# Five more chunks of the gate blocks by seven products

## The chip, the cores and the metric

The kernel runs on one core of a Trainium2 chip. The metric is the device time of one execution in microseconds (us). Before the change it is 2385.62 us, the median of three runs (2385.2 to 2386.27).

TensorE (PE) multiplies matrices into PSUM, VectorE (DVE) and ScalarE (ACT) work element by element, GpSimd (POOL) issues some of the transfers, and SyncE (SP) issues the loads of weights. All engines run beside each other and wait for one another by semaphores.

## The reference

One decoder layer on 256 tokens of width 2048: a half-step SwiGLU FFN, then a mixer with two branches (sparse attention with an indexer, and an RG-LRU recurrence), then a second FFN, with layer norms between. What matters here is the part between the projections and the merging of the branches:

```python
q, k, v, qi, ki, wi, rx, rg, gates = split_cols(h @ w_in[l])
y_attn = dsa_attention(q, k, v, qi, ki, wi)
g_attn, g_rnn = jnp.split(jax.nn.sigmoid(gates), 2, axis=-1)
merged = g_attn * (y_attn @ w_attn_branch[l]) + g_rnn * (y_rnn @ w_rnn_branch[l])
```

The product for `gates` has K = 2048 and 4096 columns. The kernel computes it as eight blocks of 512 columns, `gate_block(0)` to `gate_block(7)`.

## The kernel before

**Products.** Activations are held with features on the partitions and serve as the stationary operand, 128x128 at a time; weights move past them. Both are float32 split into a high and a low half, and a product takes three terms (`three`, L637 to L639): high by high, high by low, low by high. `W.unit` hands out the weights in order. A weight piece (`raw`, 128x1024) is loaded by SP (L177), its high half `wh` is a copy by ACT (L228), its low half `wl` a subtraction by DVE (L229). Five pieces of `wh` and `wl` fit (`HL_BUFS`). When TensorE begins a piece, four further ones are to be split (`AHEAD`) and eight to be loaded; the raw pieces have four buffers.

**Plain and fast chunks.** K has sixteen tiles of 128, and a chunk is four of them. A plain chunk of a block of 512 columns is two pieces ("c"), and each K tile is multiplied for both halves of the tokens (t = 0, 1) with 512 columns: 4 x 2 x 3 = 24 matmuls. A fast chunk treats two token halves, two halves of the columns and pairs of K tiles as 2x2 blocks and needs seven products in place of eight, with 256 columns each: 7 x 2 x 3 = 42 matmuls. Its weights come as one load of 128x2048 (`rf`, two buffers), of which four pieces are made: "p1q3" (DVE sums 1024 columns into `ws`, L191), "p2" (a sum of 512, L195), "q5p7" (a sum of 512, L198) and "q4p6" (no sum). Three of these have 1024 columns and one has 512, and each is split by L228 and L229. The sums on the activations' side are the `forms` (tiles `sh`, `sl`), made once for chunks 2 and 3 of this stage (`FAST_A`) and used by the projection blocks before.

**PSUM.** A plain block sums into two `mm` buffers, one for each token half. A block with a fast chunk takes two more, of the four `bp` buffers, from its first fast piece until `joined` (L1135 to L1141) has added the seven products up: a copy by ACT, four sums of 256 columns and two of 512 by DVE. `joined` writes two `stg` tiles; without fast chunks ACT's tanh (L1281) reads `mm` itself.

**The order around the change.** After the FFN come nine projection blocks (`A_ORDER`; all but the first, and but the small one, with chunks 2 and 3 fast), then `gate_block(0)` to `gate_block(5)`, then four blocks of the attention branch's output (`ya`). The order on PE, SP and POOL is the order of the program; that of DVE and ACT is the scheduler's. Beside the gate blocks runs the background (`bg`): the indexer for the second token half (L1171 on PE, L1191 to L1202 on DVE) and sixteen attention heads, four at a time (`head`: scores L1215 and L1216 on PE, L1219 to L1224 on DVE, exponential L1227 on ACT, scaling L1229 and L1231 on DVE, transposes L1235 on PE, copy L1238 on ACT, value products L1241 and L1242 on PE, L1245 and L1246). Each step of these tasks is taken when TensorE begins a new piece of weights (`on_piece`), so the tasks are counted in pieces, not in time. Scores, transposes and value products of a head each take one `bp` buffer. The first four heads start in the same step; later ones one step apart. `bg.drain` after the sixth gate block would finish what is left. The gates go to memory by POOL (L1282) and are fetched for the merging after the sixth block. `left_again` (L578) prepares sums of `ya` for the next stage.

`block_plan` spreads the pieces of a block: one plain piece first, then the fast pieces with the plain ones between them. `GATE_FAST` names the fast chunks of each gate block and is read at two places, where the pieces are listed and where the block is computed.

Of the kernel before, what the change touches and what calls it, by code (L numbers as in the profile page):

```python
# [65 lines left out]
FAST_A = (2, 3)  # L66


def block_plan(chunks, fills, lead=2, n=4, late=True):

    plain = [("c", k) for q in range(n) if q not in chunks for k in (4 * q, 4 * q + 2)]
    forms = [(f, q) for q in chunks for f in FORMS]
    rest = ["o"] * fills
    plan = [(rest.pop(), 0) for _ in range(min(lead, fills))] + plain[:1]
    plain = plain[1:]
    slow = []
    while plain or rest:
        for which in (plain, rest) if late else (rest, plain):  # L80
            if which:
                p = which.pop(0)
                slow.append((p, 0) if p == "o" else p)
    if not forms:
        return plan + slow
    step = len(forms) / (len(slow) + 1)
    n = 0
    for i, f in enumerate(forms):
        plan.append(f)
        while len(slow) > n and i + 1 >= (n + 1) * step:  # L90
            plan.append(slow[n])
            n += 1
    return plan
# [14 lines left out]
FILLS = [(g, nb, 2 * p) for g, (b0, b1) in enumerate(SEGS[:-1]) for nb in range(4) for p in range(b1 - b0)]  # L108
PLANS = layer_plans()
PLAN_A = block_plan(FAST_A, 0, 0)  # L110
GATE_FAST = ((), (), (), (3,), FAST_A, FAST_A, (), ())
YA_FAST = ((), (0, 1), (0, 1), (0, 1))
YR_FAST = ((0, 1), (0, 1), (0,), (0,))
MG_FAST = ((), (0, 1), (0, 1))
# [185 lines left out]
def tile_layer(ctx, tc, x_fm, x_tm, pos, f1a, f1o, wA, wki, wB, wG, lru, wab, wrb, wo, f2a, f2o,  # L300
# [43 lines left out]
    def block_pieces(ap, plan, fills=None, fo=None):  # L344
        chunk = {}
        for f, k in plan:
            if f == "c":
                pieces.append((ap[:, k * 512:k * 512 + PIECE], None))
            elif f == "o":
                g, nb, k = next(fills)  # L350
                k += 2 * SEGS[g][0]
                pieces.append((fo[nb][:, k * 512:k * 512 + PIECE], None))
            else:
                if k not in chunk:
                    chunk[k] = ap[:, k * 2048:(k + 1) * 2048]
                pieces.append((chunk[k], f))
# [18 lines left out]
    for b in range(6):  # L375
        block_pieces(wG[b], block_plan(GATE_FAST[b], 0, 0))
    for b in range(4):
# [8 lines left out]
    for b in range(6, 8):  # L386
        block_pieces(wG[b], block_plan(GATE_FAST[b], 0, 0))
    for b in range(4):
# [882 lines left out]
    def product(x, forms, fast):  # L1271

        c, e = blockF(x, forms, block_plan(fast, 0, 0, len(x) // 4), None)
        return (joined(c, e), True) if e else (c, False)

    def gate_block(b):
        s, own = product(hs, gate_forms, GATE_FAST[b])
        dst = (ga + gr)[b]
        for t in range(2):
            u = s[t] if own else U("gt")  # L1280
            A.activation(u, s[t], AF.Tanh, scale=0.5)  # L1281
            G.dma_start(dst[t], u)  # L1282
# [220 lines left out]
```

## Time and profile before

| | us |
|---|---|
| Time, median of three runs | 2385.62 |
| Span of the profiled execution | 2383.7 |
| What lies around the span, by the median | 1.9 |
| PE busy in the span | 2367.7 |
| DVE busy in the span | 2212.6 |
| ACT busy in the span | 1504.0 |
| The six gate blocks beside the heads (906.2 to 1070.6 us) | 164.4 |
| PE busy in them | 163.84 |
| DVE busy in them | 136.01 |
| ACT busy in them | 96.42 |

The profile is of one execution, whose span runs from the first to the last instruction; its own time isn't listed beside the three runs, which lie 1.5 to 2.6 us above the span. A busy time is the time in which at least one instruction of the engine runs: matmuls overlap their successors, so the distance of two starts, not the duration of one, is what a matmul costs, and the same holds in smaller measure for DVE. The idle time of an engine is put down to what ended it. The granted clock of TensorE is 1.000 over the whole span.

### The profile page before, as it was taken

The numbers are of one execution on the slowest core, as the hardware profiler recorded it, in microseconds if no ns is written. First come the engines' busy times: TensorE is split into PE (matmuls) and PEld (weight loads), VectorE is DVE, ScalarE is ACT, GpSimd is POOL, SyncE is SP. The second block draws the span as 40 slices with busy tenths as digits, with TensorE's granted clock in tenths as the row PEclk, the third lists the DMA queues.
The fourth block names the chain that finished last, engine by engine and source line by source line (L and its number), as shares of the span: only waits on it lengthen the run. The fifth ranks groups of instructions, "written<-read, shape, count | busy, mean of one in ns | idle before, by whom it ended". The sixth has DMA issues, their size and how long they took to land.

```text
span 2383.7 us, 38855 instructions
## 1 busy us (share of the span) xinstructions
PE 2367.7 (99%) x14926; PEld 2115.5 (89%) x14926; DVE 2212.6 (93%) x3130; ACT 1504.0 (63%) x2048; POOL 124.0 (5%) x196
## 2 busy tenths in 40 slices
PE   9999999999999999999999999999999999999999
PEld 7898999989988888888999998888888899999997
DVE  8999999999999998789788888998999999999997
ACT  7666666666647554665588885555766666666663
POOL 0000000000000000001000001100000000000000
PEclk9999999999999999999999999999999999999999
DMA  8666666666666456547655568755676666676665
GB/s 302 194 226 210 219 212 227 215 213 212 201 206 221 177 186 183 185 142 264 207 184 184 190 187 295 254 191 179 213 221 216 217 211 196 230 230 207 215 214 178
DMA packets 123163, 501.26 MB, mean 210 GB/s; under 512 B 14272, under 2 KB 14528, under 8 KB 102112
## 3 DMA queue, kind: packets, MB, share of 16 engines
q1 hardware_dynamic: 104400, 454.60, 54.9%
q0 software_dynamic: 18576, 44.17, 8.0%
q8 instruction: 117, 1.92, 0.3%
q14 instruction: 70, 0.57, 0.1%
HBM read 467.26 MB, written 10.49 MB: 200 GB/s over the span
## 4 chain that ended last, share of the span: by engine, by line
PE 94%; DVE 4%; issue 1%; DMA 0%; ACT 0%; POOL 0%; POOLq 0%; SPq 0%; DVEq 0%; ACTq 0%
PE mm L637 21%; PE mm L639 21%; PE mm L638 21%; PE bp L638 6%; PE bp L637 6%; PE bp L639 6%; PE mm L1337 4%; PE mm L1335 4%; PE mm L1336 4%; DVE wl L229 2%; PE bp L1027 1%; DVE ws L191 0%; PE bp L1216 0%; PE bp L1115 0%; PE bp L1171 0%
## 5 line engine op out<-in xcount | busy, mean ns | idle before, releaser
L228 ACT ACTIVATE wh<-raw 128x1024 fp32r<-128x1024 f32 (+2 forms) x538 | 550.1, 1044 | 286.6 <-PE mm L639 162.4
L229 DVE TENSOR_TENSOR wl<-raw,wh 128x1024 fp32r<-128x1024 f32 (+2 forms) x538 | 635.0, 1197 | 95.0 <-ACT wh L228 93.1
L228 ACT ACTIVATE wh<-rf 128x1024 fp32r<-128x1024 f32 (+1 forms) x489 | 440.2, 915 | 314.4 <-PE mm L639 155.4
L229 DVE TENSOR_TENSOR wl<-rf,wh 128x1024 fp32r<-128x1024 f32 (+1 forms) x489 | 506.2, 1042 | 11.7 <-ACT wh L228 6.0
L637 PE MATMUL mm<-wh,hs 128*128 128x512 f32 (+1 forms) x884 | 317.0, 359 | 0.0
L639 PE MATMUL mm<-wh,hs 128*128 128x512 f32 (+1 forms) x884 | 311.1, 352 | 1.2 <-DVE hs L818 1.2
L638 PE MATMUL mm<-wl,hs 128*128 128x512 f32 (+1 forms) x884 | 310.8, 352 | 0.1
L639 PE MATMUL mm<-wh,g 128*128 128x512 f32 (+1 forms) x696 | 274.5, 394 | 0.0
L637 PE MATMUL mm<-wh,g 128*128 128x512 f32 (+1 forms) x696 | 274.4, 394 | 0.0
L638 PE MATMUL mm<-wl,g 128*128 128x512 f32 (+1 forms) x696 | 274.4, 394 | 0.0
L228 ACT ACTIVATE wh<-ws 128x1024 fp32r<-128x1024 f32 x163 | 173.0, 1061 | 141.1 <-PE mm L639 77.0
L637 PE MATMUL bp<-wh,sh 128*128 128x256 f32 x918 | 258.6, 282 | 0.0
L638 PE MATMUL bp<-wl,sh 128*128 128x256 f32 x918 | 256.5, 279 | 1.3 <-DVE wl L229 1.3
L639 PE MATMUL bp<-wh,sl 128*128 128x256 f32 x918 | 256.2, 279 | 0.0
L191 DVE TENSOR_TENSOR ws<-rf 128x1024 f32<-128x1024 f32 x163 | 198.6, 1218 | 7.6 <-DMA rf<-f1a 2.1
L229 DVE TENSOR_TENSOR wl<-ws,wh 128x1024 fp32r<-128x1024 f32 x163 | 198.5, 1218 | 2.8 <-ACT wh L228 2.6
L639 PEld LDWEIGHTS mm<-wh,hs 128*128 128x128 f32 x884 | 165.9, 188 | 27.5 <-DVE hs L818 2.6
L637 PEld LDWEIGHTS mm<-wh,hs 128*128 128x128 f32 x884 | 166.0, 188 | 24.3 <-issue 1.5
L638 PEld LDWEIGHTS mm<-wl,hs 128*128 128x128 f32 x884 | 166.1, 188 | 22.5 <-DVE wl L229 0.7
L1337 PE MATMUL mm<-hs,wl 128*128 128x256 f32 x640 | 179.8, 281 | 0.0
L1335 PE MATMUL mm<-hs,wh 128*128 128x256 f32 x640 | 179.8, 281 | 0.0
L1336 PE MATMUL mm<-hs,wh 128*128 128x256 f32 x640 | 179.8, 281 | 0.0
(341 smaller groups left out, 5327.0 us busy)
## 6 DMA issues: line engine op xcount, KB each, us to landing
rf<-f1a SPq DMA_DIRECT2D x64, 1024.0 KB, 5.6
rf<-f2a SPq DMA_DIRECT2D x64, 1024.0 KB, 5.8
raw<-f1o SPq DMA_DIRECT2D x88, 512.0 KB, 6.6
raw<-f2o SPq DMA_DIRECT2D x88, 512.0 KB, 6.7
raw<-wB SPq DMA_DIRECT2D x80, 512.0 KB, 4.2
raw<-wG SPq DMA_DIRECT2D x54, 512.0 KB, 4.3
raw<-f2a SPq DMA_DIRECT2D x48, 512.0 KB, 4.6
raw<-f1a SPq DMA_DIRECT2D x47, 512.0 KB, 5.4
```

The source lines that it names most:

```text
L191: v.tensor_tensor(t, b[:, 0:4:3], b[:, 1:2].to_broadcast([P, 2, 2, 256]), op=OP.add)
L228: nc.scalar.activation(hp, src, AF.Copy)
L229: self.last = nc.vector.tensor_tensor(lp, src, hp, op=OP.subtract)
L637: T.matmul(ps, xh, w[0], start=start, stop=False)
L638: T.matmul(ps, xh, w[1], start=False, stop=False)
L639: T.matmul(ps, xl, w[0], start=False, stop=stop)
L1027: T.transpose(ps[:, k * S + t * P:k * S + (t + 1) * P], z[:, t * 512 + k * P:t * 512 + (k + 1) * P], ident)
L1335: T.matmul(ps[:, :S], w[0], x[:, 0], start=first, stop=False)
L1336: T.matmul(ps[:, :S], w[0], x[:, 1], start=False, stop=False)
L1337: T.matmul(ps[:, :S], w[1], x[:, 0], start=False, stop=last)
```

## The change

One tuple changes. It says for each of the eight gate blocks which chunks of K are fast.

```diff
-GATE_FAST = ((), (), (), (3,), FAST_A, FAST_A, (), ())
+GATE_FAST = ((3,), (3,), FAST_A, FAST_A, FAST_A, FAST_A, (), ())
```

Blocks 0 and 1 take chunk 3 by seven products, block 2 chunks 2 and 3, and block 3, which had chunk 3 already, chunk 2 as well: five chunks more. In blocks 0 to 2 the `joined` path takes the place of the direct one. The pieces of a block follow from its plan: 8 without a fast chunk, 10 with one, 12 with two. The left-hand forms of chunks 2 and 3 exist already.

## The prediction

> **What bounds the kernel now.** I read the page first: the busy line of each engine, then the engines of the chain that ended last, then the two kinds of weight transfer.
>
> ```profile
> PE 2367.7 (99%) x14926; PEld 2115.5 (89%) x14926; DVE 2212.6 (93%) x3130; ACT 1504.0 (63%) x2048; POOL 124.0 (5%) x196
> PE 94%; DVE 4%; issue 1%; DMA 0%; ACT 0%; POOL 0%; POOLq 0%; SPq 0%; DVEq 0%; ACTq 0%
> rf<-f1a SPq DMA_DIRECT2D x64, 1024.0 KB, 5.6
> raw<-wG SPq DMA_DIRECT2D x54, 512.0 KB, 4.3
> ```
>
> TensorE carries 94% of the chain; VectorE, at 93% busy, is close behind. What decides is therefore the stretch that the change touches. I call the gate blocks G0 to G5 and cut the windows view where the timeline shows each block's last product. The columns are length, then busy time of PE, PEld, DVE, ACT and POOL with counts, clock, DMA share, GB/s.
>
> ```profile
> 906.20:933.50 27.30, 27.30 (x129) 20.63 (x129) 22.77 (x48) 13.51 (x18) 0.00 (x0) 1.00 0.63 196
> 933.50:959.20 25.70, 25.70 (x121) 21.06 (x120) 20.39 (x44) 13.12 (x21) 1.08 (x2) 1.00 0.62 182
> 959.20:988.30 29.10, 29.10 (x142) 24.24 (x141) 22.68 (x52) 16.80 (x41) 1.07 (x2) 1.00 0.56 182
> 988.30:1015.10 26.80, 26.44 (x154) 22.96 (x153) 22.03 (x47) 17.59 (x41) 1.08 (x2) 1.00 0.59 197
> 1015.10:1049.50 34.40, 34.21 (x213) 30.35 (x212) 29.63 (x58) 21.97 (x46) 1.07 (x2) 1.00 0.37 138
> 1049.50:1070.60 21.10, 21.10 (x135) 18.91 (x134) 18.51 (x22) 13.42 (x15) 1.07 (x2) 1.00 0.45 138
> sum 164.40, PE 163.84 PEld 138.16 DVE 136.01 ACT 96.42 POOL 5.39; mean PE 27.31 PEld 23.03 DVE 22.67 ACT 16.07 POOL 0.90
> ```
>
> PE is idle for 0.56 us of 164.40, so a product less is time gained. DVE is idle for 28.4 us: that is the cover on which the change draws. For a stretch where this cover is already used up, the same view over the fast projection blocks (745.5 to 906.2 us) ends in this sum:
>
> ```profile
> sum 160.70, PE 159.26 PEld 141.44 DVE 158.09 ACT 94.27 POOL 0.00; mean PE 22.75 PEld 20.21 DVE 22.58 ACT 13.47 POOL 0.00
> ```
>
> There DVE is 98.4% busy and PE still loses only 1.44 us of 160.70. The waits of PE from 700 to 1160 us name the three kinds of loss that follow here as well:
>
> ```profile
> PE bp L638 <- DVE wl L229: 0.7, 1, 0.7
> ...
> PE bp L1115 <- ACT rl L1182: 0.6, 1, 0.6
> PE bp L1215 <- DVE ya L1246: 0.4, 1, 0.4
> ```
>
> The first is a weight half that DVE made too late; the other two are a PSUM buffer of the `bp` kind not yet read out.
>
> **TensorE's side.** First and last of 23 consecutive 512-wide products, then of 24 consecutive 256-wide ones, from the timeline of PE:
>
> ```profile
> 914.44 0.39 PE L638 MATMUL mm<-wl,hs 128*128 128x512 f32 x1
> ...
> 919.57 0.40 PE L639 MATMUL mm<-wh,hs 128*128 128x512 f32 x1
> 903.28 0.28 PE L637 MATMUL bp<-wh,sh 128*128 128x256 f32 x1
> ...
> 905.96 0.28 PE L639 MATMUL bp<-wh,sl 128*128 128x256 f32 x1
> ```
>
> The pitch is 5.13/22 = 0.2332 us for 512 columns and 2.68/23 = 0.1165 us for 256. A plain chunk (four K tiles, two token halves, three terms) is 24 x 0.2332 = 5.60 us; a fast one (seven products, two K tiles each, three terms) is 42 x 0.1165 = 4.89. I take 0.70 saved, five times: **-3.5 us**. (A block's products then take 22.4 us plain, 21.7 with one fast chunk, 21.0 with two.) That is 0.15%. The most that the change can give is thus under 0.2%, about what a measurement of this kernel can tell from no change.
>
> **VectorE's side.** One stretch of DVE's timeline holds the kinds of instruction that a fast chunk needs, each starting as the one before it lets it (L198, the third sum, has L195's 512 columns):
>
> ```profile
> 1052.45 0.42 DVE L1138 TENSOR_TENSOR stg<-bp,stg 128x256 f32<-128x256 f32 x1
> 1052.78 0.41 DVE L1139 TENSOR_TENSOR stg<-bp,stg 128x256 f32<-128x256 f32 x1
> 1053.12 1.27 DVE L1141 TENSOR_TENSOR stg<-stg,mm 128x512 f32<-128x512 f32 x2
> 1054.31 1.22 DVE L229 TENSOR_TENSOR wl<-rf,wh 128x1024 fp32r<-128x1024 f32 x1
> 1055.44 1.22 DVE L229 TENSOR_TENSOR wl<-raw,wh 128x1024 fp32r<-128x1024 f32 x1
> 1056.58 1.22 DVE L191 TENSOR_TENSOR ws<-rf 128x1024 f32<-128x1024 f32 x1
> 1057.71 1.22 DVE L229 TENSOR_TENSOR wl<-rf,wh 128x1024 fp32r<-128x1024 f32 x1
> 1058.85 0.68 DVE L195 TENSOR_TENSOR rf<-ws,rf 128x512 f32<-128x512 f32 x1
> 1059.45 0.68 DVE L229 TENSOR_TENSOR wl<-rf,wh 128x512 fp32r<-128x512 f32 x1
> 1060.05 1.22 DVE L229 TENSOR_TENSOR wl<-raw,wh 128x1024 fp32r<-128x1024 f32 x1
> ```
>
> By the distance of the starts, 1024 columns cost 1.135 us, 512 cost 0.60, 256 cost 0.335. A plain chunk is two subtractions, 2.27. A fast one is the sums (L191 1.135, L195 0.60, L198 0.60) and three and a half subtractions (3 x 1.135 + 0.60): 6.34. Each chunk adds 4.07, five 20.3; a block's weights take 9.08 plain, 13.15 with one fast chunk, 17.2 with two. G0, G1 and G2 had no fast chunk and now need `joined` (four of 256, and L1141 twice, 1.19): 2.53 each, 7.6. Together **+27.9 us of DVE**, against 28.4 idle. ACT gets 1.5 more copies of 1024 per chunk and three small ones, some 9 us at about DVE's lengths, beside 68 idle: I cost them at nothing; were that cover gone, DVE's subtractions behind them would be late too.
>
> The sum over six blocks just fits, but it is not evenly spread. The background tasks take one step per piece of weights, and a fast chunk has four pieces where a plain one has two. G0 to G5 had 8, 8, 8, 10, 12, 12 pieces and now have 10, 10, 12, 12, 12, 12. The heads' first scores come at the 14th step and their last product at the 45th:
>
> ```profile
> 948.40 0.38 PE L1215 MATMUL bp<-hT,hT 128*128 128x128 f32 x2
> ...
> 961.29 0.55 DVE L1231 TENSOR_SCALAR s<-s,s 128x128 f32<-128x128 f32 x2
> 962.23 1.47 PE L1235 MATMUL bp<-ident,s 128*128 128x128 f32 x12
> ...
> 1043.66 0.38 PE L1242 MATMUL bp<-pT,stg 128*128 128x128 f32 x2
> ```
>
> They ended late in G4; now all of them, and the index scores before them, fall into G0 to G3. That is where DVE is short. Through G2 (32 steps) I count as follows. DVE's work other than products was 22.77 - 9.08 - 2.53 (the join of the block before) = 11.2 in G0, 20.39 - 9.08 = 11.3 in G1, 22.68 - 9.08 = 13.6 in G2, and eight of ten steps of G3, 0.8 x (22.03 - 13.15) = 7.1: 43.2. The blocks' own work is 2 x 13.15 + 17.2 and three joins, 51.1. DVE needs 94.3. PE needs 2 x 21.7 + 21.0 for products, and for the rest, its busy time less the old products, 27.3 - 22.4 = 4.9, 3.3, 6.7 and 0.8 x (26.44 - 21.7): 83.1. **DVE is short by 11.2 us at the end of G2.** What is left for G3 is 0.2 x 8.9 of its own other work and G4's 29.63 - 17.2 - 2.53 = 9.9, which with 17.2 and a join makes 31.4, against PE's 0.2 x 4.7 + (34.21 - 21.0) + 21.0 = 35.1; in G4 and G5 it is 19.7 against 21.0. So what comes later wins time back for DVE, but PE's waits are spent by then.
>
> Two things soften this. Sums for the next stage were pulled forward as filler and can go back after G3:
>
> ```profile
> L578 DVE TENSOR_TENSOR t<-ya 128x256 f32<-128x256 f32 x8 | 3.2, 415 | 0.0
> ```
>
> At 0.33 each they take 2.6. And DVE enters G0 four pieces ahead; if it lends three, at 13.15/10 to 17.2/12, about 1.4 each, that is 4.2. So 11.2 - 2.6 - 4.2 = 4.4 us in which PE waits. From below the bound is nothing (the whole lead is lent and the tasks slip past their steps unharmed, as in the projection stage); from above 11.2.
>
> **PSUM, loads, queues.** A fast block holds two of the four `bp` buffers from its second piece to its join. The first four heads go in step: their scores, transposes and value products each take all four, and now find two. On PE's hand-written order everything queues behind: the two later heads, and the block's own products. From the rows above each such wait is 0.4 to 0.6 us; three groups of two give up to 3 us, from nothing. It lies in G1 and G2, where DVE is short anyway, and a stall there lets DVE catch up, so I add only 0.1. Five transfers of 1024 KB replace ten of 512 KB on SP, the bytes are the same, and the DMA share of 0.56 to 0.63 in G0 to G3 leaves room; I cost that at nothing, hidden by the loads' eight pieces of lead. A late one would cost DVE the 1.3 us by which the larger lands later, once or twice. The output path (ACT's tanh, POOL's store) is read only after G5.
>
> **The sum**: -3.5 + 4.5 = +1.0 us. On the profiled execution this is 2383.7 to 2384.7. The median, 2385.62, is 1.92 above that span; carried over, **2386.6 us**.
>
> **A rule that speaks against.** The timeline shows 256 columns at exactly half the pitch of 512, though each product brings its own weight load:
>
> ```profile
> L639 PEld LDWEIGHTS mm<-wh,hs 128*128 128x128 f32 x884 | 165.9, 188 | 27.5 <-DVE hs L818 2.6
> ```
>
> The load, at 188 ns, is longer than the pitch of 116.5, so loads overlap. The Trainium skill, page "TensorE: Matmul & The Clock Gate", section "Back-to-back issue gap", holds that in a stream of load and product the spacing is set by both, so that short products cost more per column (81 ns for 128 columns, 131 for 512). This trace disagrees (0.1165 us against 0.2332); by the rule a fast chunk would save less than the 0.70 above, and rival 3 prices its extreme from the rows.
>
> **Rivals.**
> 1. *The cover holds.* As in the projection stage (98.4% busy, 1.44 lost), lead and filler take the whole shortage; PE waits 0 to 2.4 us. Time 2382.1 to 2384.5. For it: that stage. Against it: there the load was even, without sixteen heads.
> 2. *VectorE takes over as the bound, in G1 and G2.* The lead doesn't help, because a head's scale (961.29) is needed by PE's transposes at 962.23, hardly a microsecond later, whatever weights lie ready. Then the 11.2 are paid: -3.5 + 11.2 = +7.7, 2393.3; with the filler moved away +5.1, 2390.7. It decides, as a slowdown over 0.2%, from 8.3 us of waiting.
> 3. *The weight load sets the pace of short products.* At 188 ns a fast chunk would be 42 x 0.188 = 7.9 against 5.6, five times +2.3: 2397. The pitch above speaks against it.
> 4. *It doesn't do what it says,* because the left-hand forms for these chunks are late or the order elsewhere shifts. The projection blocks used the same forms before. Time about 2385.6, either side.
>
> **How the numbers follow.** Forecast (2384.5 to 2388.5) 0.50; rival 1 0.24; rival 2 0.22 (2388.5 to 2394); rival 3 0.01; rival 4 0.03. Faster by over 0.2% (under 2380.8) needs more than the products can give: 0.02, out of rival 4. Slower (above 2390.4): two thirds of rival 2, and rival 3: 0.16. Within 0.2%: 0.82. The range 2382.5 to 2392.0 leaves out the last of rival 1 and the upper part of rival 2.
>
> **What would show it.** Right: 15 products fewer at 0.2332 us, DVE over 95% busy from G0 to G3, the last head's value product at G4's first pieces, and some 4 us of new waits of PE on `wl` (L229) or on `bp` in G1 and G2. Wrong: PE idle under 2 us there (rival 1); over 8 us, mostly ended by DVE (rival 2); a 256-wide pitch above 0.12 (rival 3); or new gaps outside G0 to G5.

## The result, and the profile after

The changed kernel takes 2404.01 us (median of five runs, 2401.56 to 2405.99) against 2385.32 before: ratio 1.0077, interval 1.0065 to 1.0089. It is 18.7 us slower. The profiled execution has a span of 2402.2 us and a time of 2404.24. First the same lines of the page of after: busy time of each engine, and the chain by engine.

```profile
PE 2371.0 (99%) x15016; PEld 2121.7 (88%) x15016; DVE 2238.0 (93%) x3173; ACT 1513.4 (63%) x2061; POOL 123.9 (5%) x196
PE 54%; DVE 3%; issue 1%; ACT 0%; POOL 0%; POOLq 0%; ACTq 0%; DVEq 0%
```

The averages hide it: PE is still 99% busy. The chain's shares add up to only 58% of the span here (99% before): it was not followed back to the start, so its 54% for PE is no fall of PE's share and says nothing of the loss. The timeline puts the first product of the stage behind the gate blocks at 1088.64 us (1070.48 before), and the index scores ahead of G0 at 905.96 (906.17): the stretch has grown from 164.31 to 182.68 us, by 18.4. The whole loss lies there. The windows view of after (columns as in the prediction: length, busy times, clock, DMA share, GB/s):

```profile
906.00:940.40 34.40, 34.40 (x191) 28.04 (x191) 33.91 (x70) 19.84 (x27) 1.08 (x2) 1.00 0.50 150
940.40:950.20 9.80, 2.22 (x14) 1.66 (x12) 9.37 (x23) 1.06 (x1) 0.00 (x0) 0.80 0.76 289
950.20:956.40 6.20, 6.16 (x19) 5.21 (x20) 4.67 (x12) 3.17 (x6) 0.00 (x0) 0.50 0.00 0
...
1038.00:1042.00 4.00, 4.00 (x13) 3.19 (x12) 0.67 (x2) 0.49 (x1) 0.00 (x0) 0.57 0.54 222
...
sum 182.60, PE 166.88 PEld 144.22 DVE 161.71 ACT 105.99 POOL 5.38; mean PE 23.84 PEld 20.60 DVE 23.10 ACT 15.14 POOL 0.77
```

Up to 940.4 nothing has gone wrong: PE is busy throughout, DVE 99%. Then PE works for 2.2 us of 9.8, and when it goes on, its clock is granted at a half. The waits of PE in after, from 900 to 1085 us (line, releaser, total us, times, longest):

```profile
PE bp L1215 <- DVE s L1219: 7.6, 1, 7.6
PE bp L1235 <- DVE ya L1246: 2.0, 1, 2.0
PE bp L1241 <- DVE stg L1136: 1.4, 1, 1.4
PE bp L1235 <- ACT pT L1238: 1.2, 1, 1.2
PE bp L1235 <- DVE s L1231: 1.1, 3, 0.4
PE bp L1215 <- ACT pT L1238: 0.9, 1, 0.9
PE bp L1241 <- DVE ya L1246: 0.8, 1, 0.8
PE bp L1215 <- DVE ya L1246: 0.6, 1, 0.6
```

They are ten waits in eight groups, 15.6 us by these rounded rows. Every one belongs to the attention heads; none is for weights (`wl`, L229). The largest in PE's timeline of after:

```profile
923.06 1.14 PE L1171 MATMUL bp<-kiT,hT 64*128 64x256 f32 x8
...
940.49 0.38 PE L1215 MATMUL bp<-hT,hT 128*128 128x128 f32 x2
...
942.02 0.60 PE L1216 MATMUL bp<-hT,hT 128*128 128x256 f32 x2
950.24 0.80 PE L1215 MATMUL bp<-hT,hT 128*128 128x128 f32 x2 [7.62 <-DVE s L1219]
...
952.97 0.63 PE L637 MATMUL mm<-wh,hs 128*128 128x512 f32 x1
953.39 0.63 PE L638 MATMUL mm<-wl,hs 128*128 128x512 f32 x1
...
956.64 0.39 PE L637 MATMUL mm<-wh,hs 128*128 128x512 f32 x1
956.88 0.39 PE L638 MATMUL mm<-wl,hs 128*128 128x512 f32 x1
```

Three heads' scores went into PSUM, so of the four `bp` buffers the block held only one at this time, not the two that the text above and the prediction count from its first fast piece. The fourth head stood for 7.62 us until DVE read out the first (L1219). Behind it, 512-wide products start 0.42 us apart, and from 956.4 on 0.24. What DVE did, in its timeline of after:

```profile
945.25 0.43 DVE L1196 MAX8 s<-score 128x8 f32<-128x256 f32 x1
...
946.31 1.23 DVE L191 TENSOR_TENSOR ws<-rf 128x1024 f32<-128x1024 f32 x1
947.46 0.42 DVE L1196 MAX8 s<-score 128x8 f32<-128x256 f32 x1
947.79 0.67 DVE L195 TENSOR_TENSOR rf<-ws,rf 128x512 f32<-128x512 f32 x1
...
949.22 0.29 DVE L1202 TENSOR_TENSOR bias<-bias,tri 128x128 f32<-128x128 f32 x1
949.62 1.02 DVE L1219 SCALAR_TENSOR_TENSOR s<-bp,bias 128x384 f32<-128x384 f32 x2
```

The read-out adds the mask of the selected keys, and the mask was finished (L1202) only at 949.5. Its own steps (such as L1196) are short and stand among sums and splits of weights. The same two marks, last index score and finished mask, in the kernel before:

```profile
926.77 1.14 PE L1171 MATMUL bp<-kiT,hT 64*128 64x256 f32 x8
...
943.82 0.29 DVE L1202 TENSOR_TENSOR bias<-bias,tri 128x128 f32<-128x128 f32 x1
```

Before, the mask took 17.3 us from the last index score and was ready 4.3 us ahead of the heads' first score (948.40). After, it takes 26.4 us, and the first score comes 17.4 us after the last index score in place of 21.6: the mask is 9.0 us late. Of this swing of 13.3 us, 9.1 is the mask's own lengthening and 4.2 the earlier arrival of the heads. What lengthened it can be read from DVE's work between the marks. Before, that was six subtractions of weights (L229, 7.3 us) and four of the indexer's sums (L1191, 1.9). After, it is nine subtractions (10.4), three sums of weights (2.6), the join of G0 (2.9) and nine of the indexer's sums (4.3): some 11 us more.

The 18.4 us add up as follows. PE's idle time in the stretch is 182.60 - 166.88 = 15.7 us, against 0.6. The clock's share of 0.80, 0.50 and 0.57 in the three windows stands for some 10.2 us and 3.4 us at a half; 6.2 us of the first and all of the second fell on products, which costs half of each, 4.8 us. The products save 3.5. So 15.1 + 4.8 - 3.5 = 16.4; 2.0 us are not assigned. (The 4.8 is an estimate from the clock's share; run e12 below tests its first part.)

### The profile page after: what moved, and what is told of

Its sections match the earlier page's. It is cut to its first block, busy times and chain, and to the rows that moved or that the text cites. A ratio compares the mean times of both kernels' runs of the same rounds, so it can differ in the third digit from the quotient of the medians.

```text
span 2402.2 us, 39075 instructions
## 1 busy us (share of the span) xinstructions
PE 2371.0 (99%) x15016; PEld 2121.7 (88%) x15016; DVE 2238.0 (93%) x3173; ACT 1513.4 (63%) x2061; POOL 123.9 (5%) x196
## 4 chain that ended last, share of the span: by engine, by line
PE 54%; DVE 3%; issue 1%; ACT 0%; POOL 0%; POOLq 0%; ACTq 0%; DVEq 0%
PE mm L639 11%; PE mm L638 11%; PE mm L637 11%; PE mm L1336 4%; PE mm L1335 4%; PE mm L1337 4%; PE bp L638 3%; PE bp L639 3%; PE bp L637 3%; DVE wl L229 1%; DVE ws L191 0%; PE bp L1027 0%; ACT wh L228 0%; DVE rf L195 0%; DVE rf L198 0%
## 5 line engine op out<-in xcount | busy, mean ns | idle before, releaser
L228 ACT ACTIVATE wh<-raw 128x1024 fp32r<-128x1024 f32 (+3 forms) x528 | 539.7, 1043 | 269.5 <-PE mm L639 145.1
L229 DVE TENSOR_TENSOR wl<-raw,wh 128x1024 fp32r<-128x1024 f32 (+3 forms) x528 | 622.6, 1196 | 82.3 <-ACT wh L228 80.0
L228 ACT ACTIVATE wh<-rf 128x1024 fp32r<-128x1024 f32 (+1 forms) x504 | 453.7, 915 | 336.2 <-PE mm L639 175.5
L229 DVE TENSOR_TENSOR wl<-rf,wh 128x1024 fp32r<-128x1024 f32 (+1 forms) x504 | 520.9, 1040 | 19.2 <-ACT wh L228 13.4
L637 PE MATMUL mm<-wh,hs 128*128 128x512 f32 (+1 forms) x864 | 307.9, 356 | 0.0
L639 PE MATMUL mm<-wh,hs 128*128 128x512 f32 (+1 forms) x864 | 302.4, 350 | 1.2 <-DVE hs L818 1.2
L638 PE MATMUL mm<-wl,hs 128*128 128x512 f32 (+1 forms) x864 | 302.2, 350 | 0.2 <-DVE wl L229 0.2
L228 ACT ACTIVATE wh<-ws 128x1024 fp32r<-128x1024 f32 x168 | 178.3, 1061 | 143.1 <-PE mm L639 79.8
L637 PE MATMUL bp<-wh,sh 128*128 128x256 f32 x948 | 267.4, 282 | 0.0
L229 DVE TENSOR_TENSOR wl<-ws,wh 128x1024 fp32r<-128x1024 f32 x168 | 204.1, 1215 | 2.2 <-ACT wh L228 2.1
L638 PEld LDWEIGHTS bp<-wl,sh 128*128 128x128 f32 x948 | 178.3, 188 | 3.9 <-DVE wl L229 1.9
L637 PEld LDWEIGHTS bp<-wh,sh 128*128 128x128 f32 x948 | 178.2, 188 | 2.3 <-issue 0.3
L1335 PE MATMUL mm<-hs,wh 128*128 128x256 f32 x640 | 179.8, 281 | 0.0
```

The costliest lines, as they stand in the source:

```text
L228: nc.scalar.activation(hp, src, AF.Copy)
L229: self.last = nc.vector.tensor_tensor(lp, src, hp, op=OP.subtract)
L637: T.matmul(ps, xh, w[0], start=start, stop=False)
L638: T.matmul(ps, xh, w[1], start=False, stop=False)
L639: T.matmul(ps, xl, w[0], start=False, stop=stop)
L1335: T.matmul(ps[:, :S], w[0], x[:, 0], start=first, stop=False)
```

## The experiments

Three theories were tried against each other. *Mask, cadence*: the background takes a step with each piece of weights, and the fast chunks' short pieces drive the heads ahead of the work that they wait for. *Load (sum)*: DVE's 27.9 us of added work. *Buffers*: a fast block holds `bp` buffers, of which four heads in step need four. Each run's own text says which it could tell apart. Medians; "before" on the same chips was 2385.3 to 2385.8.

| run | us | ratio to before, interval |
|---|---|---|
| e1 heads five pieces later | 2397.28 | 1.0050, 1.0035 to 1.0065 |
| e2 two chunks, G2 and G3 | 2388.40 | 1.0013, 1.0004 to 1.0022 |
| e3 two chunks, G0 and G1 | 2398.80 | 1.0058, 1.0041 to 1.0074 |
| e6 first heads apart | 2394.36 | 1.0038, 1.0023 to 1.0053 |
| e7 e1 and e6 | 2393.16 | 1.0032, 1.0019 to 1.0046 |
| e8 DVE lighter | 2393.94 | 1.0035, 1.0022 to 1.0048 |
| e9 before, with the steps | 2395.62 | 1.0046, 1.0031 to 1.0061 |
| e10 before, with the buffers held | 2390.54 | 1.0023, 1.0013 to 1.0032 |
| e11 three heads at a time, later | 2402.28 | 1.0067, 1.0052 to 1.0082 |
| e12 spare products in the gap | 2401.59 | 1.0065, 1.0050 to 1.0080 |
| e13 before, three heads at a time | 2388.22 | 1.0011, 1.0001 to 1.0020 |
| e14 pair, heads first: before, after | 2415.90, 2416.47 | 1.0127, 1.0112 to 1.0142; 1.0129, 1.0112 to 1.0146 |
| e16 e7 and e8 | 2393.12 | 1.0031, 1.0019 to 1.0043 |
| e18 cadence as before | 2397.63 | 1.0052, 1.0039 to 1.0065 |
| e19 e18 and e6 | 2394.25 | 1.0038, 1.0026 to 1.0050 |
| e20 e18 and e8 | 2387.97 | 1.0011, 1.0002 to 1.0021 |
| e21 e18, e8 and e6 | 2386.92 | 1.0007, 0.9998 to 1.0016 |

### Where the time goes: which blocks, which wait

**e2_g23 and e3_g01** split the change.

```diff
-GATE_FAST = ((3,), (3,), FAST_A, FAST_A, FAST_A, FAST_A, (), ())
+GATE_FAST = ((), (), (3,), FAST_A, FAST_A, FAST_A, (), ())        # e2
+GATE_FAST = ((3,), (3,), (), (3,), FAST_A, FAST_A, (), ())        # e3
```

> Only G2 (chunk 3) and G3 (chunk 2) become fast, G0 and G1 stay plain as in the kernel before: two chunks, 10.7 of the 27.9 us of DVE work. Mask theory: the pieces of G0 and G1 are unchanged, so the first scores come when they came before, no wait over 2 us and no clock dip; time 2383 to 2388. Sum theory, in proportion to DVE's work: 2385.3 + 0.38 x 18.7 = 2392. Buffer theory: the first scores meet a plain block with four free buffers, as before; like the mask theory, 2383 to 2388.

> Only G0 and G1 (chunk 3 each) become fast: two chunks and two joins, 13.2 of the 27.9 us of DVE work. Mask theory: the wait at the fourth score comes back nearly whole, 5 to 8 us, with the clock at a half for some 6 us behind it; with 1.4 us saved, 2393 to 2399. Sum theory, in proportion: 2385.3 + 0.47 x 18.7 = 2394, but in many waits under 2 us each. Buffer theory: like the mask theory at the fourth score.

Two chunks in G2 and G3 cost 2.8 us, two in G0 and G1 13.2. In e3 the wait at the fourth score is back (5.9 us), with a clock of 0.71 and 0.60 in the two windows of 5 us behind it. (These windows run from 945 to 955 us; the first holds the end of the wait.) That is the mask's side of both forecasts, up to e2's 0.4 us above its range. A fixed price per microsecond of DVE work is ruled out: 10.7 us of it cost 2.8, and 13.2 us cost 13.2. The buffer theory gave the same forecasts and isn't tested by this pair.

**e12_busy** fills the gap.

```diff
+        if h == 3:
+            w, full = hs[0][:, 0, :P], hs[0].rearrange("p a t -> p (a t)")
+            spare = MM()
+            for i in range(26):
+                T.matmul(spare, w, full, start=i == 0, stop=i == 25)
         ps = BP()
         T.matmul(ps[:, :P], q[:, :P], k[:, :P], start=True, stop=True)
```

> The changed kernel, with 26 spare 512-wide products (6.1 us, into a free mm buffer that nobody reads) issued on PE just ahead of the fourth head's first score, where it stood idle for 7.6 us. Clock theory (the idle stretch lets the granted clock fall to a half for 10.2 us, of which 6.2 hit products): PE's idle there shrinks to some 1.5 us, the clock stays at 1.00 until G3, and the time falls by 3.1 us to about 2401. If the half clock has another cause: the dip stays and the time is 2403 to 2405.

PE's timeline of e12 at that place:

```profile
942.23 6.27 PE L1218 MATMUL mm<-hs 128*128 128x512 f32 x26
950.24 0.49 PE L1220 MATMUL bp<-hT,hT 128*128 128x128 f32 x2 [1.74 <-DVE s L1224]
```

The score comes at the same moment as in after, 950.24. The clock is 1.00 from 935 to 960, so the half clock there followed from PE standing idle. The time is 2401.59, 2.4 us less than the changed kernel although PE does 6 us of useless work; the forecast was 3.1. That difference is not clear of noise by the runs alone (2400.25 to 2404.19 against 2401.56 to 2405.99), but the two profiles agree with it: the stage behind the gate blocks starts at 1086.37 us in place of 1088.64.

**e14_before and e14_after** take the heads away from the gate blocks in both kernels.

```diff
     for h in range(NH):
         bg.add("head", head(h), 4)
+    bg.drain("rope", "qk", "head")
```

> The kernel before, with the index scores and all sixteen heads finished ahead of the gate blocks, with nothing of PE's beside them: one of a pair with the next. Both theories: tens of us slower than 2385.6, since the heads' chain of waits is no longer covered; in G0 to G5 PE has no waits and takes the products' own 130.9 us.

> The changed kernel with the heads finished ahead of the gate blocks in the same way. Heads theory (the five chunks cost only by what they do to the heads beside them): 3.5 us faster than its pair, within 1 us, PE without waits over 1 us in G0 to G5 although DVE does 27.9 us more there. Load theory (DVE can't feed the five chunks in any case): no faster than its pair, with PE waiting on wl (L229).

The windows view from the first product of G0 to the first of the next stage, of e14_before and then of e14_after:

```profile
970.80:1101.80 131.00, 131.00 (x670) 110.06 (x669) 82.88 (x86) 64.15 (x70) 5.39 (x10) 1.00 0.61 198
```

```profile
973.50:1101.00 127.50, 127.50 (x759) 112.10 (x758) 108.38 (x126) 73.22 (x83) 5.39 (x10) 1.00 0.57 196
```

The five chunks save 3.50 us, and PE waits for nothing, although DVE has 25.5 us more to do and is 85% busy. The forecast for the whole time failed: e14_after is 0.6 us slower than its pair and not 3.5 faster. Its heads' part ahead of G0 ended 2.7 us later, and the profiles lose another 0.9 us behind the stretch (spans of 2415.1 and 2415.0); neither was followed up. Within the blocks the saving is real, and DVE feeds the five chunks without a wait of PE. So the loss needs the heads beside them; DVE's added work alone doesn't make it.

### What makes the heads wait: one part alone

**e9_steps** gives the kernel before nothing but steps, two more in each of G0 and G1, taken together at the block's start; **e10_hold** gives it nothing but held buffers.

```diff
+        for _ in range(2 if b < 2 else 0):          # e9, in gate_block
+            bg.step()
         s, own = product(hs, gate_forms, GATE_FAST[b])
```

```diff
+            if i == 1 and hold:                     # e10, in blockF, for G0 to G2
+                held = [BP(), BP()]
+                for b in held:
+                    T.transpose(b[:, :P], ident, ident)
...
+        for b in held:
+            A.activation(U("hold")[:, :P], b[:, :P], AF.Copy)
```

> The kernel before, all its plain chunks kept, but G0 and G1 each take two steps of the background more, as they do with a fast chunk: no DVE work added, no bp buffer held. Step theory: the heads come too early and PE waits for them, 4 us or more at one place, 2391 to 2399. Load theory: the mask keeps its 17 us and the index scores come earlier too, so the first scores find it almost ready; PE waits 0 to 2 us at the first transposes, 2385 to 2389.

> The kernel before, all plain chunks kept, but G0, G1 and G2 each hold two bp buffers from their second piece to their end (two small transposes write them, two small copies on ACT read them). Buffer theory (four heads in step need four bp buffers): waits at the first scores, transposes and value products of the heads, together 5 to 10 us, 2391 to 2399. Load theory: the mask is ready in time as before, each read-out follows in half a microsecond, and the waits are 1 to 3 us together: 2386 to 2389.

Both miss the load theory's forecast: 10.0 us and 4.9 us slower, without a fast chunk more. In e9 the mask is nearly in time (ready at 940.2, first score at 939.92), and the loss comes later. The timeline of e9, PE and ACT:

```profile
963.03 0.38 PE L1242 MATMUL bp<-pT,stg 128*128 128x128 f32 x2
...
969.53 0.46 PE L1215 MATMUL bp<-hT,hT 128*128 128x128 f32 x2 [3.32 <-DVE ya L1246]
```

```profile
965.55 1.29 ACT L1283 ACTIVATE gt<-mm 128x512 f32<-128x512 f32 x2 [3.66 <-PE mm L639]
966.74 1.05 ACT L228 ACTIVATE wh<-raw 128x1024 fp32r<-128x1024 f32 x1
967.69 1.20 ACT L1245 ACTIVATE ya<-bp 128x256 fp32r<-128x256 f32 x4
```

The first four heads' value products were done by 963.4, but their read-out (L1245) stood on ACT behind the gate's tanh, which waited 3.66 us for the end of the block. PE then waited 3.32 us for the buffers, the largest of 6.6 us of waits in this run. The steps had moved the value products to the end of a block, where a fixed order on ACT puts something slow ahead of them. In e10 the waits are small (1.2 at the scores, 0.7 at the transposes, 1.7 at the value products) and the clock stays at 1.00: shorter than the buffer theory's 5 to 10, longer in effect than the load theory's. At the first scores e10 also holds more than the changed kernel does: only two scores went in before the first read-out (949.40), the third at 950.01. So its 4.9 us are not the price of the buffers in the changed kernel.

**e8_nosums** takes load off DVE and leaves the rest. It leaves out the sums of weights of all ten fast chunks, five of which were fast before, so its results are not the layer's. DVE's busy time in the stretch falls to 141.3 us, against 161.8 in after and 136.1 before.

```diff
         b = self.raw[k].rearrange("p (r j c) -> p j r c", r=2, j=4)
+        if k in self.bare:                          # chunks of G0 to G5
+            return {"p1q3": b[:, 0:4:3], "p2": b[:, 2:3], "q5p7": b[:, 1:3], "q4p6": b[:, 0:2]}[form]
```

> All five chunks with the same pieces, products, buffers and steps, but the sums of weights in the gate blocks' ten fast chunks are left out (the seven products run on unsummed weights): 10 x 2.33 = 23.3 us less work on DVE. The mask took 26.4 us from the last index score to its end (17.3 before), with DVE at 98%. Load theory (DVE's load stretches the mask and the heads' read-outs): the mask takes 17 to 20 us again, no wait over 2.5 us at the first scores, 2382 to 2388. Step theory (the pieces come too fast for heads and buffers, whatever DVE carries): a wait of 4 us or more at the first scores, 2393 to 2400.

The timeline of e8, DVE and PE:

```profile
945.08 0.29 DVE L1209 TENSOR_TENSOR bias<-bias,tri 128x128 f32<-128x128 f32 x1
```

```profile
946.09 0.49 PE L1222 MATMUL bp<-hT,hT 128*128 128x128 f32 x2 [3.37 <-DVE s L1226]
```

10.1 us are won back. The mask takes 22.2 us (26.4 in after), and the wait shrinks from 7.6 to 3.4. Neither theory has it alone: with DVE 23.3 us lighter the heads still come before the mask.

### Cures

**e1_delay, e6_stagger, e7_both** move the heads; DVE, pieces and buffers stay.

```diff
+        for _ in range(5 if t else 0):              # e1, e7: in indexer
+            yield
         done.add(t)
```

```diff
+        for _ in range(h if h < 4 else 0):          # e6, e7: in head, after its wait
+            yield
```

> All five chunks stay fast; the heads are only held back five pieces longer after the second index mask is issued. Mask theory (PE issued the first four heads' scores at the 14th piece, before DVE had finished the mask that their read-out needs, and the fourth score stood for want of a bp buffer): no wait over 2 us at the first scores (7.6 before), clock 1.00 from G1 to G2, PE idle in the six blocks under 9 us (15.7 before), time 2387 to 2394. Sum theory (DVE simply has 27.9 us more work): DVE's work is unchanged, so 2402 to 2406 and waits of the same total at other places. Buffer theory (four heads in step against two or three free bp buffers, whenever they come): still a wait of 4 us or more at the third or fourth score, 2397 to 2404.

> All five chunks; the first four heads start one piece apart (the first at the 14th piece as before), so that their scores ask for one bp buffer at a time. Buffer theory: the wait at the scores goes, and the heads' other groups meet no shortage: PE idle under 8 us, 2387 to 2394. Mask theory: the mask is still late by some 8 us at the first score; two or three scores stand in PSUM for it, and PE waits at the third or fourth score or at the first transposes, 2 to 6 us: 2392 to 2401. Sum theory: 2402 to 2406.

> All five chunks; the heads both held back five pieces and the first four started one piece apart. Held back alone gave 2397.3, one apart alone 2394.4. If late mask and short bp buffers are two causes, each left in one of these, both cures together leave PE waits under 5 us and no clock dip: 2384 to 2389. If instead DVE's load as such sets the time, the two cures don't add: 2391 to 2397.

e1 missed its forecast: the first scores still wait 2.6 us, transposes 2.8, and four more groups 3.3 together. The heads now come 27.9 us after the last index score, but the mask slips too, to 30.3 us, and is still 2.3 us late. e6 fits the mask theory's range, and the fourth score still waits, for 3.2 us. Together they leave 2393.2, not the 2384 to 2389 of two causes that add up; this lies in the range that the forecast gave to DVE's load as such.

**e11_three and e13_three_before** run three heads at a time (e11 also holds them back four pieces, as e1 does).

```diff
-        bg.add("head", head(h), 4)
+        bg.add("head", head(h), 3)
```

> All five chunks; the heads start four pieces later and run three at a time in place of four, so that they ask for fewer bp buffers at once and reach into G4, where DVE has room. Buffer-and-order theory (PE's waits are for bp buffers whose read-out stands late in the fixed order of ACT or DVE): waits under 4 us together, no clock dip, the saved products come through: 2382 to 2388. Load theory (DVE's 27.9 us more set the time): 2391 to 2396, as with the cures so far.

> The kernel before, its heads three at a time in place of four: a control for e11. Both theories: no new waits over 1 us, 2384 to 2387; what it differs from 2385.6 is the price of three at a time alone.

e11 was expected to cure and did not; its waits of PE:

```profile
PE bp L1237 <- DVE s L1233: 6.2, 6, 2.5
PE bp L1217 <- DVE s L1221: 4.8, 1, 4.8
```

The transposes now wait for the scaling on DVE, and the first scores for the mask as before. The control is 2.4 us slower, a little above its forecast, so three at a time costs by itself.

**e18_cadence, e19_cadence_apart**: the changed kernel with the old number of steps.

```diff
-            self.on_piece()
+            if self.cur not in self.quiet:          # p2 and q4p6 of the five new chunks
+                self.on_piece()
```

> All five chunks, but of the four pieces of each newly fast chunk only two (p1q3 and q5p7) take a step of the background, so that G0 to G5 have 8, 8, 8, 10, 12, 12 steps as in the kernel before; DVE's work and the bp buffers are those of the changed kernel. Cadence theory (a step per piece drives the heads faster than ACT and DVE can read them out): the 7.6 us wait and the half clock go; what is left is the buffers' part (5.0 us in e10) less the 3.5 saved: 2385 to 2389. Load theory (DVE's 27.9 us more beside the heads): the mask is still late by several us, 2392 to 2400.

> As e18, and the first four heads start one piece apart, so that they never ask for four bp buffers in one step. Cadence and buffers as the two causes: waits under 2 us together, 2382 to 2385.5, at or below the kernel before. Load theory: no better than e18, 2392 to 2400.

e18 gives 2397.6, the load theory's side. The heads come 22.3 us after the last index score, near the 21.6 of before, but the mask takes 28.6: the fourth score waits 4.8 us. e19 spreads it out; there is no half clock and the longest wait is 1.4 us, yet 2394.3.

**e16_nosums_both, e20_cadence_light, e21_all_three** combine e8 with e7, with e18, and with e18 and e6; no other edit.

> All five chunks; both cures of e7 (heads held back five pieces, the first four one piece apart) and the sums of weights in the gate blocks left out as in e8, so that DVE has 23.3 us less to do. Load and order together: with DVE light and the heads apart nothing stands late, waits under 3 us, 2382 to 2387. Order theory alone (the fixed order of ACT and DVE against PE's, whatever the load): 2390 to 2394, like e7 and e8 each.

> e18's cadence (two steps per newly fast chunk) and e8's lighter DVE (the sums of weights in the gate blocks left out, 23.3 us) together; bp buffers as in the changed kernel. If cadence and load are the two causes beside the buffers: the first scores wait 0 to 2 us (e10 alone had 1.2), no half clock, 2384 to 2389. If they don't add: 2392 to 2396, as e8 and e18 each.

> As e20, and the first four heads one piece apart as in e6: cadence, load and buffers all eased. If these three are the whole: waits under 2 us together and the 3.5 us saved come through, 2382 to 2385. If something else costs time beside the heads: no better than e20.

e16 stays at 2393.1: with the heads held back, the lighter DVE gives nothing more, although the mask is ready 4.7 us ahead of the first score. e20 falls to 2388.0, in its range. The mask (23.4 us) is now 1.1 us behind the first score, the four scores no longer wait, and the clock is 1.00 throughout the stretch. e21 comes to 2386.9, 1.5 us above before, which is not clear of noise (interval 0.9998 to 1.0016). All its waits of PE in the stretch:

```profile
PE bp L1230 <- ACT pT L1253: 1.5, 2, 0.9
PE bp L1250 <- ACT pT L1253: 1.2, 2, 0.9
PE bp L1256 <- DVE stg L1149: 0.9, 1, 0.9
PE bp L650 <- DVE stg L1152: 0.2, 1, 0.2
```

They total 3.8 us, more than the 2 expected and about the 3.5 that the products save. So e18 removes 6.4 us of the change's cost, e8 10.1 and both 16.0. The cost is 18.7 us and the 3.5 that the products save, 22.2 together: cadence and load are most of it, and 6.2 us stay in e20, which still has 4.3 us of waits. Over all the runs the mask's length follows DVE's load: 16.3 to 17.3 us where G0 and G1 have no fast chunk (before, e2, e9, e10, e13), 22.2 to 23.4 without the sums (e8, e16, e20, e21), 24.8 to 30.3 in the others that keep the heads beside the blocks. e21 leaves the sums of weights out, so it is not a version of the kernel. None of the runs that compute the layer was faster than the kernel before.

## Why the prediction was wrong

The forecast was 2386.6 in a range of 2382.5 to 2392.0; 2404.0 lies far above. The step that failed is the price of a wait for a `bp` buffer: put at 0.4 to 0.6 us and 0.1 us in all, it was 7.62 us at one place and 15.6 in total. By the prediction's steps:

- **TensorE's side**: right. 0.70 us a chunk, 3.5 in all; e14 gives 3.50, and the pitches are the same.
- **VectorE's side, the amount**: nearly right. 27.9 us forecast, 25.5 in e14's blocks.
- **VectorE's side, where it is short**: the place was right, the heads' steps nearly so: the first scores came at the 14th, the last value product at 1045.0, ahead of G3's last piece and so one step before the forecast. The price was not. The prediction let PE wait 4.4 us for weights, after lending lead and filler. PE waited for no weight in these blocks; the lead did cover them. DVE's shortage showed in the heads, whose place in the order no lead covers. The forecast sign of DVE over 95% busy from G0 to G3 didn't come either: it was 99% up to 940.4 us, but 88% over the four blocks (123.4 of 140.8), because DVE stood behind PE in turn: from 900 to 1085 us its subtractions waited 16.4 us for ACT's copies (L228), and those 40.3 us for PE's products.
- **PSUM**: the step that failed. "From the rows above each such wait is 0.4 to 0.6 us" priced a wait by the time of a read-out and added 0.1 us. The read-out itself waited for the mask. Both marks stood in the profile of before: the mask was 4.3 us ahead of the first score, and the prediction itself let the heads come earlier and filled DVE. With 21.6 us cut to 17.4 and 17.3 lengthened to 26.4, the mask is 9.0 us late; three scores take 2.1 of them, a read-out adds 0.7, and 7.6 are left. All ten waits were for `bp`, 15.6 us in total where the sum had 4.5. That four heads find only two free buffers was wrong for the first scores, which found three; it would have made this wait longer, not shorter.
- **The clock**: not in the sum at all. In the stretch before, PE never stood long enough, and the clock was 1.00; the wait of 7.6 us halved it. Of the 4.8 us reckoned for both dips the first has 3.1, and filling the wait took 2.4 us off.
- **Rivals**: rival 2 was the nearest, waits behind a head's chain in G1 and G2, at 0.22. At 2393.3 it was short by the clock and by the heads' later waits, and the place that it named, the transposes behind a head's scale, had only 1.1 us (L1231). Rival 3 is out: 256-wide products kept half the pitch.

The clock's fall is what the Trainium skill, page "TensorE: Matmul & The Clock Gate", section "Part 1: The HAM clock gate (the "warmup" mystery)", leads one to expect: half rate after about 3.4 us without work, full rate after as much of it. The durations reckoned above, 10.2 and 3.4 us, are three such windows and one. The last section shows that a wait shorter than this was enough.

Still open is how the waits divide in the versions that stay at 2393 to 2394 (e7, e16, e19). There no wait is over 1.4 us, and each change of the heads' steps moves them to other places; e7 has two half-clock stretches of 3.4 us, e16 one and e19 none. That an instruction stands behind a slower one in a fixed order was seen once, in e9; that it explains the others was not tried.

## What to carry to other kernels

Work that is issued once per unit of other work moves when the units change in number or length: check each of its deadlines, not only the engines' sums. Price a wait on a buffer by what its reader waits for, back to the last link, and take the slack from two rows of the profile (here 4.3 us, for a change that took 13.3). On an engine in program order a chain's lateness is paid as soon as its buffers are full, however far ahead the weights are: a mask 9.0 us late gave a wait of 7.6 (after), one 1.1 us late gave none (e20).

## What the runs showed of the hardware

An idle TensorE lost its clock after waits well under 3.4 us. Windows of e1 show 0.66 from 955 to 960 us after a single wait of 2.6 us, and 0.83 from 970 to 980 after waits of 0.8 and 1.8 us within 4 us; in e10, waits of 1.2 and 1.7 us, some 20 us apart, left it at 1.00. In after, the second dip (0.57 from 1038 to 1042) followed a wait of 2.0 us with one of 0.45 shortly ahead. The clock recovered while products ran at half speed: 0.43 us apart at 953, 0.23 at 957.

The traces of the 20 kernels give the pattern behind this. Between the first and the last few microseconds of each run, two changes of the clock always lie a whole multiple of 3.413 us apart. Cut on that grid, a window at full clock with PE idle for 1.99 us or more was followed by a window at half clock each time, and one with 1.49 us or less never. In between both occur: it fell after 1.53 (e16) and 1.54 (e7), and stayed after 1.74 (e12) and 1.95 (e14_after). So no single long wait is needed: in e7 two of 1.31 and 1.32 us, ending at 963.95 and 966.68 us, were enough. From half clock it rose again after every window with at most 0.42 us idle. The idle times come from modelled ends of matmuls, so the limits are those of this profile.
